# A hybrid attention and recurrence layer on one core: load order at the start, order of the gates, query blocks by twos, small products on both halves

## The chip, the cores and the metric

The kernel runs on one core of a Trainium2 chip. The metric is the time of one execution on the device, in microseconds (us), and less is better. TensorE (PE in the profile), VectorE (DVE), ScalarE (ACT), GpSimd (POOL) and SyncE (SP, which here only issues transfers) each work through a queue of their own and wait for each other through semaphores.

## What is computed

One layer of a decoder over 512 tokens of width 1024, all in float32. Cut to what matters here:

```python
xn = rmsnorm(x, norm_gain)
aq, ak, av, ag, bq, bf, bi, bg, gate_a, gate_b = split(xn @ w_in)      # 8 pieces of 512, 2 of 1024
q, k = rmsnorm(heads(aq)), rmsnorm(heads(ak))                          # 8 heads of 64
ya = softmax(q @ k.T / 8 + bias[q_pos - k_pos], causal) @ heads(av)    # 512 tokens: all blocks are selected
ya = (ya * silu(ag)) @ w_up_a
log_f, key = gates(bf)                                                 # 4 heads of 128
yb = gated_recurrence(q=silu(bq), k=key, v=bi, decay=log_f)
yb = (rmsnorm(yb) * silu(bg)) @ w_up_b
h = x + (sigmoid(gate_a) * ya + sigmoid(gate_b) * yb) @ w_out
out = h + (p @ w_ple) * sigmoid(h @ w_ple_gate)
```

## The kernel before

**The large products.** Every projection is three products of split operands. `split` (L183, L184) makes a high part on ACT and a low part on DVE, and `mm3` (L245) or `proj_tok` (L398) multiplies high by high, low by high and high by low, 512 columns each. Weights come through a ring: SP loads a raw tile (`wf`, 2 buffers), ACT writes `wh`, DVE writes `wl` (3 buffers each), two weights ahead of use. A new `wh` can be written only when TensorE is done with the tile whose buffer it takes. The first projection (`bi`) runs on x times its gain, before x is normalised, in four steps `start(kp)`. Its first weight comes in two halves (L269, L272), the second (`wf1`) whole.

**The side work.** Between the large products, the order of TensorE's queue is written out by the program itself (`manual_schedule` for PE). The generators of `sides` (`qk_norm`, `attention`, `recurrence`) yield an estimate of time, and `tick`, called after every group of large products, lets those that are due put their small products in. So each piece of side work interrupts the large products at a place that is fixed when the program is built. The queues of DVE and ACT are ordered by a planner from priorities, and some tiles are raised with `high_priority(offset=AHEAD)`.

**Attention.** `attention` walks through 16 steps, four query blocks of 128 tokens for each of four pairs of heads. `scores` (L641) writes two banks `s` of 128 x (128 to 512), six products on two 64-row halves. DVE adds the bias and takes the maximum (L648), ACT exponentiates (L650), DVE scales (L651, L652). `transposed` (L662) turns the result `p` through TensorE into `pt`, ACT copies it (L666), and after the last block `out_values` (L678) multiplies with the values. Only two banks of PSUM carry the tag `a` of all this, and `qk_norm` uses the same two for its transposes `qtp` and `ktp` (L623), which `scale_split` (L187 on ACT into `kh`, L188 on DVE into `kl`) empties.

**The recurrence.** `head(i)` makes `bf` and `bq` and then the gates (`hgrn_gates`, L423 to L441); in the kernel before all four heads' gates come before any output gate `ag`, `bg`. `hgrn_intra` writes one chunk's scores as a tree of levels 64, 32, 16, 8, 4, 2, 1. The 64-wide products (L494) all go to output rows 0 to 63, the 32-wide ones (L497, L498) to rows 96 to 127 and 64 to 95, and `diag` (L473) makes 16 products of 32 x 32 for each smaller level, of which only the later half of each pair of blocks is used: a mask in `pred` (L480) selects it. `hgrn_out` follows with transposes `hktp` (L538), states `hds` (L546), outputs `hop` (L559, L561) and a sum of squares `hms` (L572, L573), which needs the two parts `hth` (ACT) and `htl` (DVE).

Of the kernel before, what the change touches and what calls it, by code (L numbers as in the profile page):

```python
# [24 lines left out]
GH = 4  # L25
# [4 lines left out]

HP = 4.2
AP = 9.6
# [10 lines left out]
ORDER = [("ag", 0), ("bg", 0), ("bg", 1), ("ag", 1), ("gb", 0), ("gb", 1), ("gb", 2), ("bg", 2), ("ag", 2), ("gb", 3), ("gb", 4),  # L43
         ("gb", 5), ("bg", 3), ("ag", 3), ("ga", 0), ("ga", 1), ("gb", 6), ("gb", 7), ("ga", 4), ("ga", 2), ("ga", 3),
         ("ga", 5), ("ga", 6), ("ga", 7)] + [("ub", i) for i in range(KD)]
# [7 lines left out]
def hybrid_layer_kernel(  # L53
# [28 lines left out]
            "PT0": 2, "PT1": 2, "PT2": 2, "SG": 4, "YS": 1, "VV": 8, "s32": 1, "st": 1, "ps": 8}  # L82
# [109 lines left out]
    def w_sequence():  # L192
        for g in (2, 3, None, 0, 1):
            if g is None:
                wseq.extend([(w_tr[0], KD, 128), (w_tr[4], KD, 128)])
            else:
                wseq.extend((w_tok[g, kp], 2, 512) for kp in range(4))
        for i in range(1, GH):
            wseq.append((w_tr[i], KD, 128))
            wseq.append((w_tr[4 + i], KD, 128))  # L200
        for kind, i in ORDER:
            if kind == "ub":
# [59 lines left out]

    with tc.high_priority():

        x0 = unit("H", "xr0")
        xr.append(x0)
        raw0 = unit("w", "wf0", shape=(128, 2, 512))
        nc.sync.dma_start(x0[:, 0:256], xT[:, 0, 0:256])
# [152 lines left out]
    def hgrn_gates(h, F, Q):  # L421
        a = unit("H", f"ha{h}")
        A.activation(a, F, AF.Abs)  # L423
        A.activation(a, a, AF.Exp, scale=-1.0)
        A.activation(a, a, AF.Ln, bias=onec[:, 0:1])
        um = unit("H", f"hu{h}")
        V.tensor_scalar(um, F, -1.0, 30.0, op0=OP.mult, op1=OP.min)
        A.activation(um, um, AF.Exp)
        A.activation(um, um, AF.Ln, bias=onec[:, 0:1], scale=lbv[:, h:h + 1])
        V.scalar_tensor_tensor(a, F, 0.0, a, op0=OP.min, op1=OP.subtract)  # L430
        kb = unit("H", f"hk{h}")
        V.tensor_tensor(kb, a, F, op=OP.subtract)
        A.activation(kb, kb, AF.Exp, bias=ln1mlb[:, h:h + 1])
        G.tensor_tensor(a, a, um, op=OP.add)
        cum = um
        for c in range(NT):
            s_ = slice(c * 128, c * 128 + 128)
            V.tensor_tensor_scan(cum[:, s_], onec.to_broadcast([128, 128]), a[:, s_], 0.0, OP.mult, OP.add)
        q = a
        sigmoid(q, Q)  # L440
        V.tensor_tensor(q, q, Q, op=OP.mult)  # L441
        hg[h] = (kb, q, cum)

    def hgrn_intra(h):
# [24 lines left out]
        def diag(dst, l, r):  # L469
# [5 lines left out]
            cost(0.4)  # L475
# [3 lines left out]
        def pred(li, src):  # L479
            V.copy_predicated(s32, mk[:, li, None, :].to_broadcast([128, NT, 32]), src)  # L480
# [18 lines left out]
        cost(0.45)  # L499
# [4 lines left out]
        A.activation(sc[0:64, :, 64:128], big[0:64], AF.Copy)  # L504
        A.activation(sc[0:32, :, 32:64], big[96:128, :, 0:32], AF.Copy)
        A.activation(sc[64:96, :, 96:128], big[64:96, :, 0:32], AF.Copy)
# [6 lines left out]
        for i, k_ in enumerate(ks):  # L513
            diag(lpa[:, 1 + i], k_, k_)
# [85 lines left out]
    def qk_norm(name, banks, g, res):  # L600
# [19 lines left out]
        for i in range(HPAIRS):  # L620
            tp = bank("a", f"{name}tp{i}")
            for t in range(NT):
                PE.transpose(tp[:, t * 128:t * 128 + 128], raws[t][:, i * 128:i * 128 + 128], ident)  # L623
            cost(0.44)
            scale_split(hs[i], ls[i], tp, g)
            res.append((hs[i], ls[i]))
            yield 1.3
        done.add(name)

    def attention(qn, kn, va, sags, res):  # L630
        def scores(hp, qb, T):
            (qh, ql), (kh, kl) = qn[hp], kn[hp]
            nk = 128 * (qb + 1)
            qs = slice(qb * 128, qb * 128 + 128)
# [7 lines left out]
            cost(3 * max(0.107, nk * 0.00042))  # L642
            with tc.high_priority(offset=AHEAD):
                for j in range(2):
                    sp = sps[j]
                    pr = unit("P", f"p{hp}{qb}{j}")
                    st = unit("ps", f"ps{hp}{qb}{j}", shape=(128, 4))
                    V.tensor_tensor_reduce(pr[:, :nk], sp[:, :nk], T[j][:, nk - 1::-1], -1.0, 3e38,  # L648
                                           OP.add, OP.min, st[:, 0:1])
                    A.activation(pr[:, :nk], pr[:, :nk], AF.Exp, bias=st[:, 0:1], scale=-1.0, accum_out=st[:, 1:2])  # L650
                    V.reciprocal(st[:, 2:3], st[:, 1:2])  # L651
                    V.tensor_scalar(pr[:, :nk], pr[:, :nk], st[:, 2:3], None, op0=OP.mult)  # L652
# [3 lines left out]
        def transposed(hp, qb, prs):  # L656
            nk = 128 * (qb + 1)
            pts = []
            for j in range(2):
                tp = bank("a", f"pt{hp}{qb}{j}")  # L660
                for kb in range(qb + 1):
                    PE.transpose(tp[:, kb * 128:kb * 128 + 128], prs[j][:, kb * 128:kb * 128 + 128], ident)  # L662
                cost(0.11 * (qb + 1))
                pt = unit("PT" if qb == NT - 1 else f"PT{qb}", f"ptS{hp}{qb}{j}", shape=(128, nk))
                with tc.high_priority(offset=AHEAD):
                    A.activation(pt, tp[:, :nk], AF.Copy)  # L666
# [3 lines left out]
        def out_values(hp, pts):  # L670

            o = bank("a", f"o{hp}")
            for qb in range(NT):
                qs = slice(qb * 128, qb * 128 + 128)
                for kb in range(qb + 1):
                    for j in range(2):
                        h0 = hp * 128 + 64 * j
                        PE.matmul(o[64 * j:64 * j + 64, qs], va[kb][:, h0:h0 + 64],  # L678
                                  pts[qb][j][:, kb * 128:kb * 128 + 128], start=(kb == 0), stop=(kb == qb))
# [11 lines left out]
        steps = [(hp, qb) for hp in range(HPAIRS) for qb in range(NT)]  # L691
        T, prs, pts = {}, {}, {}
        for n in range(len(steps) + 2):
            if n >= 2 and steps[n - 2][1] == NT - 1:
# [3 lines left out]
                out_values(hp, [pts.pop(n - 2 - NT + 1 + i) for i in range(NT)])  # L698
            if n >= 2:
                yield AP * 0.3  # L700
            if 1 <= n <= len(steps):
                pts[n - 1] = transposed(*steps[n - 1], prs.pop(n - 1))
                yield AP * 0.3
            if n < len(steps):
                hp, qb = steps[n]
                if qb == 0:
# [6 lines left out]
                prs[n] = scores(hp, qb, [T[hp, 0], T[hp, 1]])  # L713
            yield AP * 0.4
# [8 lines left out]
    def start(kp):  # L723
        with tc.high_priority():
            if kp == 0:
                load_x(2, 3)
                first_splits()
                w_load(1)
                load_x(3, KD)
# [31 lines left out]
    for i in range(1, GH):  # L761
        head(i)

# [8 lines left out]
    for kind, i in ORDER:  # L772
        if kind == "bg":
# [134 lines left out]
```

## Time and profile before

| what | us |
|---|---|
| median of 3 runs (lowest, highest) | 488.33 (488.26, 488.42) |
| the profiled execution's own time | 488.94 |
| its span, first to last instruction | 487.2 |
| TensorE busy | 475.5 |
| VectorE busy | 301.5 |
| ScalarE busy | 266.6 |
| GpSimd busy | 30.4 |

The span is what the views of the profile cut up; the time of an execution is a little longer than its span. Busy times overlap between engines. Matmuls are pipelined, so a group of them is measured best from the start of the one before it to the start of the one behind it.

### The profile page before, as it was taken

What the parts mean: (1) busy time and instruction counts of PE and PEld (TensorE: products, weight loads), DVE (VectorE), ACT (ScalarE), POOL (GpSimd) and SP (SyncE); (2) the same over time, 40 slices, a digit from 0 to 9 for tenths busy, and PEclk for the clock granted to TensorE, in tenths of its full rate; (3) what the DMA queues carried; (4) which work ended last, traced back from release to release, by engine and by line L of the source; (5) the groups of instructions that cost most, each with busy time, mean ns of one, the idle gap of its engine ahead of it and who ended that gap; (6) DMA issues with size and microseconds to landing.
All of it is one profiled execution on the core that took longest, in us unless ns stands there. A gap on an engine that the chain in (4) does not pass through costs nothing.

```text
span 487.2 us, 7943 instructions
## 1 busy us (share of the span) xinstructions
PE 475.5 (98%) x3160; PEld 386.1 (79%) x3160; DVE 301.5 (62%) x596; ACT 266.6 (55%) x463; POOL 30.4 (6%) x43
## 2 busy tenths in 40 slices
PE   8999999999979999999999999999999999999996
PEld 6787888788757878777888788877888888888885
DVE  5849483858897966947449574364348855534332
ACT  6647573354876867758557785566324542242201
POOL 2004012103110001000100000000000000000000
PEclk9999999999999999999999999999999999999999
DMA  8432222422212131222212242014323544223211
GB/s 274 171 132 84 90 86 87 152 87 89 87 43 85 47 131 49 83 86 77 98 47 86 86 131 89 22 45 130 131 71 114 187 169 149 97 89 120 87 43 44
DMA packets 17941, 48.41 MB, mean 99 GB/s; under 512 B 2248, under 2 KB 2888, under 8 KB 17904
## 3 DMA queue, kind: packets, MB, share of 16 engines
q1 hardware_dynamic: 17616, 47.82, 28.9%
q8 instruction: 24, 0.39, 0.3%
q0 software_dynamic: 144, 0.09, 0.1%
q14 instruction: 13, 0.11, 0.1%
q10 hardware_dynamic: 144, 0.01, 0.0%
HBM read 45.79 MB, written 2.12 MB: 98 GB/s over the span
## 4 chain that ended last, share of the span: by engine, by line
PE 89%; DVE 5%; DMA 2%; ACT 2%; issue 1%; POOL 1%; SPq 0%; DVEq 0%; POOLq 0%
PE ga L245 9%; PE gb L245 9%; PE g L245 9%; PE h L245 9%; PE ak L398 5%; PE ag L245 5%; PE ub L245 5%; PE ua L245 4%; PE aq L398 4%; PE bg L245 4%; PE av L398 4%; PE bf L245 3%; PE bi L398 3%; PE bq L245 2%; PE pe L245 2%; PE s L641 2%
## 5 line engine op out<-in xcount | busy, mean ns | idle before, releaser
L183 ACT ACTIVATE wh<-wf 128x1024 fp32r<-128x1024 f32 (+1 forms) x81 | 78.1, 964 | 105.8 <-PE g L245 20.4
L184 DVE TENSOR_TENSOR wl<-wf,wh 128x1024 fp32r<-128x1024 f32 (+1 forms) x81 | 89.3, 1103 | 74.3 <-ACT wh L183 73.8
L245 PE MATMUL g<-hl,wh 128*128 128x512 f32 (+1 forms) x72 | 26.3, 366 | 0.0
L245 PE MATMUL g<-hh,wl 128*128 128x512 f32 (+1 forms) x72 | 26.3, 366 | 0.0
L245 PE MATMUL g<-hh,wh 128*128 128x512 f32 (+1 forms) x72 | 26.3, 366 | 0.0
L245 PE MATMUL gb<-xh,wh 128*128 128x512 f32 x64 | 26.3, 411 | 0.0
L245 PE MATMUL ga<-xh,wh 128*128 128x512 f32 x64 | 26.1, 408 | 0.0
L650 ACT ACTIVATE p<-p,ps 128x128 f32<-128x128 f32 (+3 forms) x32 | 17.7, 555 | 13.4 <-DVE ps L648 13.1
L245 PE MATMUL gb<-xl,wh 128*128 128x512 f32 x64 | 25.0, 391 | 0.0
L245 PE MATMUL ga<-xh,wl 128*128 128x512 f32 x64 | 25.0, 391 | 0.0
L245 PE MATMUL ga<-xl,wh 128*128 128x512 f32 x64 | 25.0, 391 | 0.0
L245 PE MATMUL gb<-xh,wl 128*128 128x512 f32 x64 | 25.0, 391 | 0.0
L245 PE MATMUL h<-ml,wh 128*128 128x512 f32 x64 | 24.9, 390 | 0.0
L245 PE MATMUL h<-mh,wl 128*128 128x512 f32 x64 | 24.9, 390 | 0.0
L245 PE MATMUL h<-mh,wh 128*128 128x512 f32 x64 | 24.9, 389 | 0.0
L666 ACT ACTIVATE ptS<-pt 128x128 f32<-128x128 f32 (+3 forms) x32 | 12.4, 435 | 14.8 <-PE pt L662 14.6
L648 DVE CUSTOM_DVE_ANT_0 p<-s,bias 128x128 f32<-128x128 f32 (+3 forms) x32 | 14.7, 487 | 7.0 <-PE s L641 7.0
L460 ACT ACTIVATE hx<-hx 128x512 f32<-128x512 f32 x24 | 14.6, 626 | 7.7 <-DVE hx L459 7.4
L806 DVE TENSOR_TENSOR hf<-h,xres 128x512 f32<-128x512 f32 x8 | 5.5, 692 | 18.1 <-PE h L245 18.1
L529 POOL COPY sc<-s 32x128 f32<-32x128 f32 x16 | 7.0, 435 | 142.9 <-DVE s L480 63.1
L245 PEld LDWEIGHTS g<-hl,wh 128*128 128x128 f32 x72 | 13.6, 189 | 2.2
L245 PEld LDWEIGHTS g<-hh,wl 128*128 128x128 f32 x72 | 13.6, 189 | 2.2
(326 smaller groups left out, 1267.0 us busy)
## 6 DMA issues: line engine op xcount, KB each, us to landing
wf<-in_w_tr_dram SPq DMA_DIRECT2D x32, 512.0 KB, 3.3
wf<-in_w_tok_dram SPq DMA_DIRECT2D x15, 512.0 KB, 3.4
wf<-in_w_up_dram SPq DMA_DIRECT2D x16, 256.0 KB, 2.6
wf<-in_w_o_dram SPq DMA_DIRECT2D x8, 512.0 KB, 3.3
wf<-in_w_g_dram SPq DMA_DIRECT2D x8, 512.0 KB, 3.4
bias<-ed SPq DMA_DIRECT2D x8, 256.0 KB, 3.7
xres<-in_xT_dram SPq DMA_DIRECT2D x8, 256.0 KB, 2.9
xr<-in_xT_dram SPq DMA_DIRECT2D x7, 256.0 KB, 6.3
```

What stands on the lines that cost most here:

```text
L183: A.activation(hi, src, AF.Copy)
L184: V.tensor_tensor(lo, src, hi.bitcast(F32), op=OP.subtract)
L245: PE.matmul(ps, a[:, k, :], b[k], start=(n == 0), stop=(n == tot - 1))
L398: PE.matmul(banks[t], a[:, s_], b[:, kk, :], start=(k == 0 and i == 0), stop=(k == KD - 1 and i == 2))
L460: A.activation(x, x, AF.Exp)
L529: G.tensor_copy(sc[s_, :, s_], s32[s_])
L641: PE.matmul(sps[j][:, :nk], a[js, qs], b[js, :nk], start=(i == 0), stop=(i == 2))
L648: V.tensor_tensor_reduce(pr[:, :nk], sp[:, :nk], T[j][:, nk - 1::-1], -1.0, 3e38, OP.add, OP.min, st[:, 0:1])
L650: A.activation(pr[:, :nk], pr[:, :nk], AF.Exp, bias=st[:, 0:1], scale=-1.0, accum_out=st[:, 1:2])
L666: A.activation(pt, tp[:, :nk], AF.Copy)
L806: V.tensor_tensor(t, ps, xres, op=OP.add)
```

## The change

**First loads.** SP's list at the start becomes: both halves of the first weight, then the third piece of x, the second weight, and the other pieces of x.

**Gates.** `ORDER` gets entries `("bf", i)`: heads 1 to 3 make `bf`, `bq` and their gates between the output gates. In `hgrn_gates` one sum goes from POOL to DVE, in `qk_norm` the squares go from POOL to ACT, and the split of `ktp` and `qtp` is raised in priority.

**Query blocks.** `STEPS` makes the first two query blocks one step: 12 steps instead of 16, and 384 columns of a bank hold both blocks.

**Small products.** The 64-wide products alternate between output rows 0 to 63 and 64 to 127, the 32-wide ones go through all four groups of 32 rows, and `diag` multiplies only the columns that the level uses (16 of 32). `pred` selects from that half alone, and the copies of the products out of PSUM become six instead of three.

```diff
+STEPS = ((0, 1), (2,), (3,))
-AP = 9.6
+AP = 12.8
-ORDER = [("ag", 0), ("bg", 0), ("bg", 1), ("ag", 1), ("gb", 0), ("gb", 1), ("gb", 2), ("bg", 2), ("ag", 2), ("gb", 3), ("gb", 4),
...
+ORDER = [("bg", 0), ("ag", 0), ("bf", 1), ("bg", 1), ("ag", 1), ("gb", 0), ("bf", 2), ("gb", 1), ("gb", 2), ("bg", 2), ("ag", 2),
+         ("gb", 3), ("bf", 3), ("gb", 4), ("gb", 5), ("bg", 3), ("ag", 3), ("ga", 0), ("ga", 1), ("gb", 6), ("gb", 7),
...
         nc.sync.dma_start(raw0[:, 1], wseq[0][0][:, 1])
-        wraw.append(raw0)
+        load_x(2, 3)
+        w_load(1)
+        load_x(3, KD)
...
-        G.tensor_tensor(a, a, um, op=OP.add)
+        V.tensor_tensor(a, a, um, op=OP.add)
...
+        def queries(t, b):
+            return t.rearrange("p (n two b) -> p n two b", two=2, b=b)[:, :, 1, :]
-                    PE.matmul(dst[32 * g:32 * g + 32, c, :], l[:, o:o + 32], r[:, o:o + 32],
-                              start=True, stop=True)
+                    d, m = dst[32 * g:32 * g + 32, c, :], r[:, o:o + 32]
+                    if b:
+                        d, m = queries(d, b), queries(m, b)
+                    PE.matmul(d, l[:, o:o + 32], m, start=True, stop=True)
...
-            o = c * 128
-            PE.matmul(big[0:64, c, :], k64[:, o:o + 64], k64[:, o + 64:o + 128], start=True, stop=True)
+            o, i = c * 128, 64 * (c % 2)
+            PE.matmul(big[i:i + 64, c // 2, :], k64[:, o:o + 64], k64[:, o + 64:o + 128], start=True, stop=True)
         for c in range(NT):
-            o = c * 128
-            PE.matmul(big[96:128, c, 0:32], k32[:, o:o + 32], k32[:, o + 32:o + 64], start=True, stop=True)
-            PE.matmul(big[64:96, c, 0:32], k32[:, o + 64:o + 96], k32[:, o + 96:o + 128], start=True, stop=True)
+            for half in range(2):
+                o, i = c * 128 + 64 * half, 64 * (c % 2) + 32 * half
+                PE.matmul(big[i:i + 32, 2 + c // 2, 0:32], k32[:, o:o + 32], k32[:, o + 32:o + 64], start=True, stop=True)
...
-        diag(lpb[:, 0], k1, k1)
-        diag(lpa[:, 0], k16, k16)
+        diag(lpb[:, 0], k1, k1, 1)
+        diag(lpa[:, 0], k16, k16, 16)
...
-            G.tensor_tensor(sq, raw, raw, op=OP.mult)
+            A.activation(sq, raw, AF.Square)
...
-            scale_split(hs[i], ls[i], tp, g)
+            with tc.high_priority(offset=AHEAD):
+                scale_split(hs[i], ls[i], tp, g)
...
-            sps = [bank("a", f"s{hp}{qb}{j}") for j in range(2)]
-            for i, (a, b) in enumerate(((qh, kh), (ql, kh), (qh, kl))):
-                for j in range(2):
-                    js = slice(64 * j, 64 * j + 64)
-                    PE.matmul(sps[j][:, :nk], a[js, qs], b[js, :nk], start=(i == 0), stop=(i == 2))
+            sps = [bank("a", f"s{hp}{qbs[0]}{j}") for j in range(2)]
+            for qb, o, nk in blocks(qbs):
+                qs = slice(qb * 128, qb * 128 + 128)
+                for i, (a, b) in enumerate(((qh, kh), (ql, kh), (qh, kl))):
+                    for j in range(2):
+                        js = slice(64 * j, 64 * j + 64)
+                        PE.matmul(sps[j][:, o:o + nk], a[js, qs], b[js, :nk], start=(i == 0), stop=(i == 2))
...
         for kind, i in ORDER:
-            if kind == "bg":
+            if kind == "bf":
+                head(i)
+            elif kind == "bg":
```

What moves in the queues is seen best in two places. The first is SP at the start of the program (`xr` is a piece of x, `wf` a raw weight). Before:

```order
L270 DMA xr_100<-in_xT_dram 128x256
L137 DMA xr_105<-in_xT_dram 128x512
L137 DMA xr_119<-in_xT_dram 128x512
L272 DMA wf_101<-in_w_tok_dram 128x512
L219 DMA wf_137<-in_w_tok_dram 128x1024
L137 DMA xr_139<-in_xT_dram 128x512
```

With the change:

```order
L272 DMA xr_100<-in_xT_dram 128x256
L139 DMA xr_105<-in_xT_dram 128x512
L274 DMA wf_101<-in_w_tok_dram 128x512
L139 DMA xr_108<-in_xT_dram 128x512
L220 DMA wf_110<-in_w_tok_dram 128x1024
L139 DMA xr_112<-in_xT_dram 128x512
```

The second half of the first weight and the third piece of x change places; what comes ahead of the second weight is the same in sum. ACT's list there, with the change (`gh` is the high part of a piece of x, `ssum` and `xsq` its squares):

```order
L189 ACTIVATE gh_143<-xr_105,sm 128x512
L185 ACTIVATE wh_135<-wf_101 128x512
L189 ACTIVATE gh_186<-xr_108,sm 128x512
L181 ACTIVATE lb<-lb 128x4
L309 ACTIVATE ssum<-xr_100 128x512
L312 ACTIVATE xsq_337<-xr_105 128x512
L312 ACTIVATE xsq_340<-xr_108 128x512
L185 ACTIVATE wh_154<-wf_110 128x1024
```

Before, `gh` of the third piece stood ahead of `wh` of the half weight, and the other rows were the same: the squares of three pieces stand ahead of the second weight's `wh` in both.

The second place is DVE's list from the third `kl` to the first scores. Before:

```order
L188 SCALAR_TENSOR_TENSOR kl_1138<-ktp_1334,sm,kh_1134 128x512
L184 TENSOR_TENSOR wl_1357<-wf_1354,wh_1356 128x1024
L261 TENSOR_TENSOR hy_1237<-hy_1237,ht_1238 128x512
L427 TENSOR_SCALAR hu_1432<-bf_1293 128x512
L188 SCALAR_TENSOR_TENSOR kl_1139<-ktp_1347,sm,kh_1135 128x512
L430 SCALAR_TENSOR_TENSOR ha_1428<-bf_1293,ha_1428 128x512
```

With the change:

```order
L190 SCALAR_TENSOR_TENSOR kl_1141<-ktp_1323,sm,kh_1137 128x512
L593 SCALAR_TENSOR_TENSOR ho_1241<-hop_1233,sm,hy_1242 128x512
L186 TENSOR_TENSOR wl_1346<-wf_1343,wh_1345 128x1024
L431 TENSOR_SCALAR hu_1418<-bf_1290 128x512
L599 TENSOR_TENSOR bg0s<-bg0s,ho_1241 128x512
L190 SCALAR_TENSOR_TENSOR kl_1142<-ktp_1336,sm,kh_1138 128x512
L434 SCALAR_TENSOR_TENSOR ha_1414<-bf_1290,ha_1414 128x512
L186 TENSOR_TENSOR ybl_1273<-bg0s,ybh_1272 128x512
L436 TENSOR_TENSOR hk_1423<-ha_1414,bf_1290 128x512
L671 ISA p_1374,ps_1375<-s_1360,bias_1356 128x128
```

Between the last two `kl` three rows stood, now four stand; the `hu` row is of the second head's gates (`bf1`), which were the third head's before. Further ahead, DVE's list no longer has the second head's gates between the states `st` and `htl`: there stands only `bg0s`, one product.

## Rows read from the trace of the kernel before

**Rows 1.** The page: busy us of each engine, share of the span, instructions.

```profile
PE 475.5 (98%) x3160; PEld 386.1 (79%) x3160; DVE 301.5 (62%) x596; ACT 266.6 (55%) x463; POOL 30.4 (6%) x43
```

**Rows 2.** Busy time by stretch: length, then each engine's busy us.

```profile
110.00:140.00 30.00, 27.43 (x229) 21.94 (x227) 26.49 (x54) 21.05 (x34) 5.64 (x8) 1.00 0.21 72
140.00:152.00 12.00, 10.02 (x49) 7.58 (x50) 10.07 (x28) 7.17 (x16) 1.29 (x1) 1.00 0.25 88
```

**Rows 3.** TensorE's waits from 100 to 160 us: total, times, longest.

```profile
PE s L641 <- DVE kl L188: 1.7, 1, 1.7
PE pt L662 <- DVE p L652: 1.2, 2, 0.7
PE hms L573 <- DVE htl L184: 1.2, 1, 1.2
PE ktp L623 <- DVE kl L188: 0.5, 1, 0.5
```

**Rows 4.** Timeline of the start: start, us, engine, instruction, [idle before, releaser].

```profile
8.56 0.63 ACT L183 ACTIVATE wh<-wf 128x512 fp32r<-128x512 f32 x1 [0.44 <-DMA wf<-in_w_tok_dram]
9.24 0.50 PE L398 MATMUL bi<-wh,gh 128*128 128x512 f32 x1 [0.68 <-ACT wh L183]
9.71 1.14 ACT L308 ACTIVATE xsq<-xr 128x512 f32<-128x512 f32 x2
10.76 1.05 ACT L183 ACTIVATE wh<-wf 128x1024 fp32r<-128x1024 f32 x1
11.83 1.23 DVE L184 TENSOR_TENSOR wl<-wf,wh 128x1024 fp32r<-128x1024 f32 x1
```

**Rows 5.** Timeline of DVE and ACT, 126 to 141 us.

```profile
126.91 1.37 DVE L438 TENSOR_TENSOR_SCAN hu<-onec,ha 128x128 f32<-128x128 f32 x4 [1.65 <-POOL ha L434]
128.19 0.67 DVE L184 TENSOR_TENSOR htl<-ht,hth 128x512 fp32r<-128x512 f32 x1
...
137.65 1.22 DVE L184 TENSOR_TENSOR wl<-wf,wh 128x1024 fp32r<-128x1024 f32 x1
...
139.98 0.75 DVE L188 SCALAR_TENSOR_TENSOR kl<-ktp,sm,kh 128x512 fp32r<-128x512 f32 x1
```

**Rows 6.** Timeline of PE around a 128-column and a 256-column run of scores.

```profile
293.98 0.39 PE L245 MATMUL ga<-xh,wl 128*128 128x512 f32 x1
...
294.46 0.28 PE L641 MATMUL s<-kh,ql 64*128 64x128 f32 x2
294.57 0.28 PE L641 MATMUL s<-kl,qh 64*128 64x128 f32 x2
...
295.11 0.39 PE L245 MATMUL ga<-xl,wh 128*128 128x512 f32 x1
...
150.53 0.39 PE L245 MATMUL bf<-xh,wl 128*128 128x512 f32 x1
...
151.74 0.40 PE L245 MATMUL bf<-xl,wh 128*128 128x512 f32 x1
```

**Rows 7.** The chain that ended last: start, us, the large products of `ua`.

```profile
362.52 21.76 PE ua L245 x96
```

**Rows 8.** Timeline of PE, small products of the first head.

```profile
92.45 0.68 PE L494 MATMUL lpb<-hx 128*64 128x64 f32 x8
...
93.14 0.20 PE L497 MATMUL lpb<-hx 128*32 128x32 f32 x1
93.15 0.20 PE L498 MATMUL lpb<-hx 128*32 128x32 f32 x1
93.17 0.20 PE L497 MATMUL lpb<-hx 128*32 128x32 f32 x1
...
93.89 0.45 PE L473 MATMUL lpa<-hx 128*32 128x32 f32 x30
```

**Rows 9.** Timeline of PE: products with 1 and with 128 moving columns, full weights.

```profile
32.35 0.95 PE L322 MATMUL mt<-onesd,ssum 128*128 128x1 f32 x8
...
118.90 0.83 PE L546 MATMUL hds<-biv,hkt 128*128 128x128 f32 x6
```

More of the change, by code (lines that the diff above doesn't have):

```diff
@@ L197, in w_sequence @@
                 wseq.extend((w_tok[g, kp], 2, 512) for kp in range(4))
-        for i in range(1, GH):
-            wseq.append((w_tr[i], KD, 128))
-            wseq.append((w_tr[4 + i], KD, 128))
         for kind, i in ORDER:
-            if kind == "ub":
+            if kind == "bf":
+                wseq.extend([(w_tr[i], KD, 128), (w_tr[4 + i], KD, 128)])
+            elif kind == "ub":
                 wseq.append((w_up[i, 1], 4, 128))
@@ L513, in hgrn_intra @@
         for i, k_ in enumerate(ks):
-            diag(lpa[:, 1 + i], k_, k_)
+            diag(lpa[:, 1 + i], k_, k_, LEVELS[1 + i])
         kd = unit("KT", f"hkd{h}")
@@ L630, in attention, with blocks, scores @@
     def attention(qn, kn, va, sags, res):
-        def scores(hp, qb, T):
+        def blocks(qbs):
+            return [(qb, sum(128 * (b + 1) for b in qbs[:i]), 128 * (qb + 1)) for i, qb in enumerate(qbs)]
+        def scores(hp, qbs, T):
             (qh, ql), (kh, kl) = qn[hp], kn[hp]
-            nk = 128 * (qb + 1)
-            qs = slice(qb * 128, qb * 128 + 128)
             prs = []
-            sps = [bank("a", f"s{hp}{qb}{j}") for j in range(2)]
-            for i, (a, b) in enumerate(((qh, kh), (ql, kh), (qh, kl))):
-                for j in range(2):
-                    js = slice(64 * j, 64 * j + 64)
-                    PE.matmul(sps[j][:, :nk], a[js, qs], b[js, :nk], start=(i == 0), stop=(i == 2))
-            cost(3 * max(0.107, nk * 0.00042))
+            sps = [bank("a", f"s{hp}{qbs[0]}{j}") for j in range(2)]
[5 more added lines that the diff above has]
+                        PE.matmul(sps[j][:, o:o + nk], a[js, qs], b[js, :nk], start=(i == 0), stop=(i == 2))
+                cost(3 * max(0.107, nk * 0.00042))
@@ L651, in scores @@
-                    V.reciprocal(st[:, 2:3], st[:, 1:2])
-                    V.tensor_scalar(pr[:, :nk], pr[:, :nk], st[:, 2:3], None, op0=OP.mult)
+                    pr = unit("P", f"p{hp}{qbs[0]}{j}")
+                    for qb, o, nk in blocks(qbs):
+                        p_ = pr[:, o:o + nk]
+                        st = unit("ps", f"ps{hp}{qb}{j}", shape=(128, 4))
+                        V.tensor_tensor_reduce(p_, sps[j][:, o:o + nk], T[j][:, nk - 1::-1], -1.0, 3e38,
+                                               OP.add, OP.min, st[:, 0:1])
+                        A.activation(p_, p_, AF.Exp, bias=st[:, 0:1], scale=-1.0, accum_out=st[:, 1:2])
+                        V.reciprocal(st[:, 2:3], st[:, 1:2])
+                        V.tensor_scalar(p_, p_, st[:, 2:3], None, op0=OP.mult)
@@ L653, in scores, with transposed @@
                     prs.append(pr)
             return prs
-        def transposed(hp, qb, prs):
-            nk = 128 * (qb + 1)
+        def transposed(hp, qbs, prs):
+            n = sum(qb + 1 for qb in qbs)
             pts = []
             for j in range(2):
-                tp = bank("a", f"pt{hp}{qb}{j}")
-                for kb in range(qb + 1):
+                tp = bank("a", f"pt{hp}{qbs[0]}{j}")
+                for kb in range(n):
                     PE.transpose(tp[:, kb * 128:kb * 128 + 128], prs[j][:, kb * 128:kb * 128 + 128], ident)
-                cost(0.11 * (qb + 1))
-                pt = unit("PT" if qb == NT - 1 else f"PT{qb}", f"ptS{hp}{qb}{j}", shape=(128, nk))
+                cost(0.11 * n)
+                pt = unit("PT" if n == NT else f"PT{qbs[0]}", f"ptS{hp}{qbs[0]}{j}", shape=(128, n * 128))
@@ L672, in out_values @@
             o = bank("a", f"o{hp}")
[L673 to L679, printed above, removed]
+            for qbs, pt in zip(STEPS, pts):
+                for qb, o0, nk in blocks(qbs):
+                    qs = slice(qb * 128, qb * 128 + 128)
+                    for kb in range(qb + 1):
+                        for j in range(2):
+                            h0 = hp * 128 + 64 * j
+                            PE.matmul(o[64 * j:64 * j + 64, qs], va[kb][:, h0:h0 + 64],
+                                      pt[j][:, o0 + kb * 128:o0 + kb * 128 + 128], start=(kb == 0), stop=(kb == qb))
             cost(1.5)
@@ L690, in attention @@
             yield lambda: {"q", "k"} <= done
-        steps = [(hp, qb) for hp in range(HPAIRS) for qb in range(NT)]
+        NS = len(STEPS)
+        steps = [(hp, i) for hp in range(HPAIRS) for i in range(NS)]
         T, prs, pts = {}, {}, {}
         for n in range(len(steps) + 2):
-            if n >= 2 and steps[n - 2][1] == NT - 1:
+            if n >= 2 and steps[n - 2][1] == NS - 1:
                 hp = steps[n - 2][0]
@@ L697, in attention @@
                     yield lambda: f"ag{hp}" in done
-                out_values(hp, [pts.pop(n - 2 - NT + 1 + i) for i in range(NT)])
+                out_values(hp, [pts.pop(n - 1 - NS + i) for i in range(NS)])
             if n >= 2:
```

53 lines of the change are left out of this document (25 added, 28 removed).

## The prediction

> **What bounds the kernel now.** I read the page first: TensorE is busy 475.5 us of the span, VectorE 62% of it, ScalarE 55%, GpSimd 6% [rows 1]. So time is saved in two ways only: TensorE gets less to do, or it waits less. Next, the busy time by stretch, to see where it waits. From 110 to 152 us it is busy 27.43 of 30 and 10.02 of 12 us, that is 4.5 us idle, and there VectorE is the full engine, with 26.49 and 10.07 us [rows 2]. TensorE's waits of that stretch name four causes, 4.6 us in all, each of them VectorE [rows 3]. The timeline of the first microseconds shows the other waits. Last I measured what one interruption of the large products costs, from the start of the large product before it to the start of the second one behind it, because a large product that follows a small one starts slower. Undisturbed, one large product takes 21.76 / 96 = 0.227 us [rows 7].
>
> The sum is made against the profiled execution's 488.94 us. It lies 0.6 us above the median of the three runs, 488.33, so 0.6 us is taken off at the end.
>
> **First loads.** The wait removed is plain: TensorE stood 0.68 us before the second half weight's first product, since `wh` of that half began at 8.56, right when its load landed [rows 4]. With the third piece of x behind it, it lands earlier. But I cost this at nothing, because of what is late next. The next products need `wl` of the second weight, and that ends at 11.83 + 1.23 = 13.06. Ahead of it, ACT's list holds the squares of three pieces of x (the last two at 9.71, for 1.14 us) and then `wh` at 10.76, for 1.05 us. The change keeps that order. The third square now waits for a piece of x that lands later, about when the half weight landed before, so ACT is not done sooner. What TensorE gains at 9.24 it waits for again at 13. The ends: 0.7 us gained, if ACT gets ahead all the same, and 0.3 us lost, if the late piece pushes the squares back. I take 0.
>
> **Two query blocks in one run.** TensorE multiplies the same columns. What goes is one run of scores and one run of transposes per pair of heads. The 128-column run costs 295.11 - 293.98 = 1.13 us less two large products, 0.45, that is 0.68; the 256-column run 151.74 - 150.53 = 1.21 less 0.45, that is 0.76 [rows 6, 7]. Joined, they cost the second run and three more pairs of 128-column products at 0.11 us (294.46 to 294.57), 1.09 us in place of 1.44. Four times 0.35 is **1.4 us saved**. The transposes are as many as before and as wide as the stream; a run fewer of them, and a score run that no longer shares its switch with a run of the recurrence, are small and of opposite signs, so I leave them at nothing (0.3 us either way). ACT copies `pt` 24 times instead of 32, which hides beside TensorE.
>
> **Products on both halves.** The 64-wide products are eight records in 0.68 us (an fp32 product is recorded twice). Less the last one's 0.22, which I estimate from the 0.20 us of the 32-wide ones, that is 0.46 us in seven gaps, 0.066 us each. The 32-wide ones go to two output groups in turn, two records in 0.03 us. The products of a level go through four groups: 30 records in 0.45 - 0.20 = 0.25 us, 0.0086 us each [rows 8]. So a record costs the same time per group, 0.03 us, and groups run side by side. On two halves I take half of 0.46 (0.23 saved), on four groups 16 records at 0.0086 in place of 0.015 (0.11 saved): 0.34 us for each of four heads, **1.4 us saved**. The ends are 0, if the halves don't overlap, and these 1.4.
>
> The Trainium skill (TensorE: Matmul & The Clock Gate, Part 3: Packing small matmuls, The mechanism) says that weight loads overlap with running matmuls only when the row group differs. By that rule this term would be 0, since both halves use all 128 rows, and the time 485.0 us. The rows just read speak against it: four groups with the same 128 rows run at a quarter of the gap of one.
>
> **Half of the columns in `diag`.** Five levels in four heads, 20 times 32 records, now move 16 columns in place of 32. At one end the gap halves: 640 x 0.0043 = 2.7 us saved. At the other it stays. The nearest rows are products with full weights: with one moving column eight records take 0.95 us, 0.12 each; with 128 columns six take 0.83 us, 0.14 each [rows 9]. Moving 128 times fewer columns takes a seventh off. What stays must be the weights, which are loaded for each record, and `diag` loads the same weights as before. I take **0**. `pred` on DVE gets shorter, the copies of `sc` on ACT become six for three; neither is waited for.
>
> **The gates and what moves off POOL.** This is the term on waits. `hms` waited 1.2 us for `htl` [rows 3]. `htl` started at 128.19, behind the second head's scan, which itself had waited 1.65 us for POOL's sum [rows 5]. The gates no longer stand there, and the sum is on DVE: this wait goes. The 0.5 us at `ktp` were DVE's full queue as well: it goes.
>
> The 1.7 us at the first scores stay. These scores need both banks of tag `a`, that is the third and the fourth `kl`. Before, `wl` started at 137.65 and the fourth `kl` at 139.98, 2.33 us later, with `wl`, `hy` and `hu` between [rows 5]. Now `wl`, `hu` and `bg0s` stand there, of the same sizes, and `ho` ahead of them: one more row, some 0.6 us. TensorE asks for the banks as late as before, six large products after the last `ktp`. So I expect 2.3 us. The fourth `kl` is raised in priority, but in the queue it still stands behind them.
>
> The 1.2 us at `pt` shrink. Nine more large products stand between scores and transposes, 9 x 0.227 = 2.0 us, while DVE gets a second block's rows and the sum `ha`. I take 0.4. Together 2.7 in place of 4.6 us: **1.9 us saved**. The ends: all waits go, 4.6 saved; or only those at `hms` and `ktp` go and the one at the scores grows, 1.1 saved.
>
> What is moved past others: head 1's weights now come behind `bg0` and `ag0` in the ring, and SP loads them in the order of use as before. The squares of `qk_norm` go to ACT, eight more activations, while ACT idles 45% of the span; the transposes that need them come 14 us of the program's own clock later, and rows 3 name no wait for them. The later heads' recurrence starts later, but 39 large products, 8.9 us, stand between its last `hms` and the products `ub` that need it.
>
> **The sum.** 0 + 1.4 + 1.4 + 0 + 1.9 = 4.7 us. 488.94 - 4.7 - 0.6 = **483.6 us**.
>
> **The rivals.**
> - The half columns pay: 2.7 us more, 480.9 us. For it: 32 columns and 32 weights are as long as each other, so either could set the gap. Against it: rows 9. Chance 0.15.
> - The middle waits stay at 4.6 us, since gates of the second head now meet the first softmax on DVE: 483.6 + 1.9 = 485.5 us. For it: VectorE is full there [rows 2], and its queue is written from estimates. Against it: two of the four waits lose their cause. Chance 0.16.
> - The halves don't overlap: 483.6 + 1.4 = 485.0 us. Against it: rows 8. The rule cited above from the Trainium skill (the same page and section) is this case. Chance 0.08.
> - Slower: each move of the output from one half to the other drains the array. Ten moves a head, 40 in all. The price of a drain by rows 6: of the 0.68 us of the 128-column run 0.33 are products, and 0.35 are the way in and out, 0.17 each. 40 x 0.17 = 6.8 us, and the 1.4 are not gained: 483.6 + 1.4 + 6.8 = 491.8 us. It would decide from 3.3 / 40 = 0.08 us a move. Against it: the 32-wide products change groups at every record within 0.01 us [rows 8]. Chance 0.04.
>
> **How the numbers follow.** Forecast 0.52, half columns 0.15, waits 0.16, halves 0.08, drains 0.04, and 0.05 for several of the lesser gains failing together, which leaves under 1 us. A measurement of this kernel can tell about 0.2%, 1.0 us, from no change. The first four cases are faster by more than that: 0.91 faster, 0.05 the same, 0.04 slower. The range runs from a little under the half columns' case, 480.6, up to 486.2, between the waits' case, 485.5, and waits and halves failing together, 486.9.
>
> **What would show it.** Scores in 12 runs; the joined run near 1.1 us. The 64-wide products at 0.03 us a record. A level's 30 records still at 0.25 us: at 0.13 the half columns pay. TensorE's waits near the second gates: none at `hms`, some 2.3 us at the first scores for `kl`. At the start no wait at 9 us and one before 13.4 for `wl`. The prediction is wrong if TensorE's idle time in the middle isn't near 2.7 us, or if the start is shorter by over 0.5 us.

## The result, and the profile after

The changed kernel takes 483.53 us (median of 4, 483.31 to 483.64) beside 488.38 us (488.26 to 488.55) before: a ratio of 0.990, with a 95% interval of 0.9883 to 0.9917. The profiled execution took 483.52 us, its span is 481.7 us. The forecast of 483.6 us holds, but not all of its terms: the one on waits came out near by errors of opposite sign, and the one on the half columns is right for another reason than it gave.

The page of the changed kernel: busy times, and the granted clock in 40 slices.

```profile
PE 473.3 (98%) x3160; PEld 386.9 (80%) x3160; DVE 300.8 (62%) x600; ACT 269.8 (56%) x475; POOL 14.1 (3%) x31
...
PEclk9999999999989999999999999999999999999999
```

Beside [rows 1], TensorE is 2.2 us less busy and GpSimd half as busy; the rest went out of waits. One slice of the clock, around 139 us, has an 8. The busy time by stretch (columns as in [rows 2]; the sixth number after the stretch's length, the one behind POOL's, is the clock):

```profile
110.00:140.00 30.00, 28.05 (x241) 22.96 (x239) 24.28 (x43) 21.07 (x35) 1.16 (x4) 0.99 0.26 89
140.00:152.00 12.00, 12.00 (x51) 9.64 (x53) 11.13 (x38) 9.05 (x22) 0.00 (x0) 0.88 0.13 39
```

TensorE is idle 1.95 us there, after 4.5 before. But in the second stretch the granted clock is 0.88. TensorE's waits in the whole span of the changed kernel:

```profile
PE s L663 <- DVE kl L190: 2.0, 1, 2.0
...
PE bi L402 <- DVE wl L186: 0.7, 2, 0.5
PE bi L402 <- ACT wh L185: 0.3, 1, 0.3
...
```

Of the four waits of [rows 3] one is left, at the first scores. The timeline of TensorE around it, and what follows:

```profile
138.87 0.32 PE L663 MATMUL s<-kh,qh 64*128 64x128 f32 x1 [1.95 <-DVE kl L190]
...
139.88 0.79 PE L246 MATMUL bq<-xh,wh 128*128 128x512 f32 x1
140.47 0.63 PE L246 MATMUL bq<-xl,wh 128*128 128x512 f32 x1
140.90 0.63 PE L246 MATMUL bq<-xh,wl 128*128 128x512 f32 x1
...
143.00 0.39 PE L246 MATMUL bq<-xl,wh 128*128 128x512 f32 x1
143.23 0.39 PE L246 MATMUL bq<-xh,wl 128*128 128x512 f32 x1
```

Behind the wait the large products start 0.43 us apart, nearly twice the usual 0.227, and from 143.0 on 0.23 again. The busy time by shorter stretches shows the clock:

```profile
139.80:143.30 3.50, 3.50 (x10) 2.73 (x10) 3.50 (x17) 2.66 (x10) 0.00 (x0) 0.55 0.00 0
143.30:148.00 4.70, 4.70 (x25) 3.91 (x24) 4.70 (x17) 3.00 (x6) 0.00 (x0) 1.00 0.02 5
```

A granted clock of 0.55 is the lower level, 1.2 GHz, for most of 3.5 us. The 27 products behind the scores start 1.53 us later than at 0.227 us each; behind other runs of scores it is 0.13 us. So the fall costs 1.4 us.

The timeline of the start (answers to [rows 4]):

```profile
8.06 0.63 ACT L185 ACTIVATE wh<-wf 128x512 fp32r<-128x512 f32 x1
8.74 0.50 PE L402 MATMUL bi<-wh,gh 128*128 128x512 f32 x1 [0.29 <-ACT wh L185]
9.96 1.14 ACT L312 ACTIVATE xsq<-xr 128x512 f32<-128x512 f32 x2
11.00 1.04 ACT L185 ACTIVATE wh<-wf 128x1024 fp32r<-128x1024 f32 x1
12.08 1.23 DVE L186 TENSOR_TENSOR wl<-wf,wh 128x1024 fp32r<-128x1024 f32 x1
13.36 0.50 PE L402 MATMUL bi<-wl,gh 128*128 128x512 f32 x1 [0.52 <-DVE wl L186]
```

TensorE goes on 0.5 us earlier, at 8.74, behind a wait of 0.29 us, but the squares, `wh` and `wl` of the second weight are each 0.25 us later. The product that needs this `wl` waits 0.52 us for it and starts at 13.36, before the change at 13.11.

The timeline of TensorE at three more places: the small products of the first head (answers to [rows 8]), the run of 96 records of three levels with the large products beside it, and a joined run of scores (answers to [rows 6]):

```profile
92.44 0.39 PE L402 MATMUL ak<-wl,xh 128*128 128x512 f32 x1
92.76 0.45 PE L507 MATMUL lpb<-hx 128*64 128x64 f32 x8
93.14 0.33 PE L511 MATMUL lpb<-hx 128*32 128x32 f32 x16
...
93.88 0.43 PE L485 MATMUL lpa<-hx 128*32 128x16 f32 x30
94.24 0.50 PE L402 MATMUL ak<-wh,xh 128*128 128x512 f32 x1
...
112.38 0.39 PE L402 MATMUL ak<-wl,xh 128*128 128x512 f32 x1
112.70 1.00 PE L485 MATMUL lpa<-hx 128*32 128x16 f32 x96
113.63 0.50 PE L246 MATMUL bg<-xh,wh 128*128 128x512 f32 x1
...
182.37 0.39 PE L246 MATMUL gb<-xh,wl 128*128 128x512 f32 x1
...
183.58 0.50 PE L246 MATMUL gb<-xh,wh 128*128 128x512 f32 x1
183.91 0.39 PE L246 MATMUL gb<-xl,wh 128*128 128x512 f32 x1
```

Eight 64-wide records take 0.45 instead of 0.68 us. Thirty records with half the columns take 0.43 instead of 0.45. The joined run takes 183.91 - 182.37 - 0.45 = 1.09 us, the forecast's number.

From here on a run of small products is costed as the start of the first large product behind it, less the start of the large product before it, less 0.227 us. So the interrupted rhythm is in it, and waits are too. The first head's run costs 94.24 - 92.44 - 0.227 = 1.58 us.

### The profile page after: what moved, and what is told of

The parts are those of the page before. It is cut to its first block, busy times and chain, and to the rows that moved or that the text cites. A ratio compares the mean times of both kernels' runs of the same rounds, so it can differ in the third digit from the quotient of the medians.

```text
span 481.7 us, 7941 instructions
## 1 busy us (share of the span) xinstructions
PE 473.3 (98%) x3160; PEld 386.9 (80%) x3160; DVE 300.8 (62%) x600; ACT 269.8 (56%) x475; POOL 14.1 (3%) x31
## 4 chain that ended last, share of the span: by engine, by line
PE 92%; DVE 4%; ACT 1%; DMA 1%; issue 1%; SPq 0%; DVEq 0%
PE gb L246 9%; PE ga L246 9%; PE g L246 9%; PE h L246 9%; PE bg L246 5%; PE ak L402 5%; PE bq L246 5%; PE ub L246 5%; PE ua L246 5%; PE aq L402 5%; PE ag L246 4%; PE av L402 4%; PE bf L246 3%; PE pe L246 2%; PE bi L402 2%; PE s L663 2%
## 5 line engine op out<-in xcount | busy, mean ns | idle before, releaser
L689 ACT ACTIVATE ptS<-pt 128x384 f32<-128x384 f32 (+1 forms) x24 | 11.6, 521 | 7.4 <-PE pt L685 7.2
L246 PEld LDWEIGHTS g<-hh,wh 128*128 128x128 f32 x72 | 13.6, 189 | 2.2
```

Of the source, the lines that this page charges most:

```text
L246: PE.matmul(ps, a[:, k, :], b[k], start=(n == 0), stop=(n == tot - 1))
L689: A.activation(pt, tp[:, :n * 128], AF.Copy)
```

## The experiments

The theory after these readings: every part is worth what the prediction says, the order of the gates makes the term on waits, the load order costs 0.3 us, and the one wait left costs more than itself through the clock. Its rivals: the halves or the joined blocks gave less and the waits more; the move of work off GpSimd, not the order, took the waits away; the half columns pay.

All the kernels are the changed one with one edit. Each result is listed with the mean clock granted to TensorE in each execution, because the fall just seen comes in some executions of a program and not in others.

**The changed kernel again.**

> The changed kernel itself, again, beside the three below on the same chip. Theory (the clock falls after the wait at the first scores in some executions and not in others): executions with a mean granted clock of 1.000 are about 1.5 us shorter than those at 0.996, near 482 us against 483.5. Rival (the clock is a matter of each program): all executions at 0.996, 483.5 within 0.3.

483.15 us (482.46 to 483.84), ratio 0.9889 (0.9876 to 0.9903). The execution at a mean clock of 0.999 took 482.46, the profiled one at 0.995 took 483.84, with 1.1 us lost behind a 1.9 us wait. Of the other two one took 483.61 at 0.995, but one only 482.7 at 0.996, so the mean clock doesn't order them fully. One kernel spreads over 1.4 us, more than most of the parts that are to be told apart, and below the traces count more than the medians.

**The query blocks one by one.**

```diff
-STEPS = ((0, 1), (2,), (3,))
-AP = 12.8
+STEPS = ((0,), (1,), (2,), (3,))
+AP = 9.6
...
-            "PT0": 2, "PT2": 2, "SG": 4, "YS": 1, "VV": 8, "s32": 1, "st": 1, "ps": 8}
+            "PT0": 2, "PT1": 2, "PT2": 2, "SG": 4, "YS": 1, "VV": 8, "s32": 1, "st": 1, "ps": 8}
```

> The changed kernel with four query blocks as four steps again, the rest as changed. Theory (a run of scores costs TensorE 0.35 us of switching besides its products): four runs more, 483.5 + 1.4 = 484.9 us, between 484.5 and 485.5 since the middle waits may shift; the 128-column run costs 0.68 us and the 256-column run 0.76, against 1.09 for the joined one. Rival (the whole gain came from the waits between 110 and 152 us, and interruptions hide): 483.5 within 0.3.

484.51 us (484.11 to 485.37), ratio 0.9921 (0.9905 to 0.9938). The four executions' clocks are 0.994 to 1.000; those at 0.999 and 1.000 took 484.1 to 484.8, some 2 us above the changed kernel's 482.46 (this trace also has 0.6 us of waits for `p`). In the trace a 128-column run costs 0.57 and a 256-column run 0.64 us, the joined one 0.98; with the 0.11 that the large product behind each loses the joining gains 0.34 us, four times, where the forecast had 0.35. The two-block transposes cost 0.58 us joined, 0.14 and 0.36 apart, and the large product behind each run loses 0.09: joined or apart is the same within 0.01 us.

**The products on one half.** The 64- and 32-wide products and their copies as before the change (one row for three):

```diff
-            PE.matmul(big[i:i + 64, c // 2, :], k64[:, o:o + 64], k64[:, o + 64:o + 128], start=True, stop=True)
+            PE.matmul(big[0:64, c, :], k64[:, o:o + 64], k64[:, o + 64:o + 128], start=True, stop=True)
```

> The changed kernel with the 64-wide products all on output rows 0 to 63 and the 32-wide ones on two groups, as before. Theory (a group of output rows takes 0.03 us a record of 32 columns, and groups run side by side): the first run of a head goes from 1.58 back to 1.91 us, four times 0.33, 484.8 us. Rival (waits alone): 483.5 within 0.3.

484.16 us (483.09 to 485.41), ratio 0.9909 (0.9889 to 0.9929). The medians alone would leave it open: executions at clocks of 0.995 to 1.000 overlap the changed kernel's. The run doesn't. TensorE at the first head's run in this kernel:

```profile
92.08 0.39 PE L402 MATMUL ak<-wl,xh 128*128 128x512 f32 x1
...
94.20 0.50 PE L402 MATMUL ak<-wh,xh 128*128 128x512 f32 x1
```

It costs 1.90 us where the changed kernel has 1.58, and the fourth head's 1.89 and 1.58. The second head's run is joined with scores and the third's with transposes: 2.79 against 2.48, and 2.79 against 2.47. So it is 0.31 to 0.32 us in all four. The wait at the scores is 2.0 us in both. So the halves do run side by side. By the rule of the Trainium skill (TensorE: Matmul & The Clock Gate, Part 3: Packing small matmuls, The mechanism), by which weight loads overlap only across row groups, there would have been no difference here. The measurement decides.

**All 32 columns, and half the weights.** The first passes no `b` to `diag`. The second loads 16 weight columns for the five levels, so their other 16 rows of scores are missing, and leaves out the copies by `pred`:

```diff
-                    PE.matmul(d, l[:, o:o + 32], m, start=True, stop=True)
+                    if b:
+                        PE.matmul(queries(dst[32 * g:32 * g + 16, c, :], b), l[:, o:o + 16], m, start=True, stop=True)
...
-        pred(4, lpb[:, 0])
```

> The changed kernel with all 32 columns in every small level, of which half are not used. Theory (the weights of each record set its gap, not the moving columns): 483.5 within 0.3 us, and 96 records of a run still cost about 1.02 to 1.05 us. Rival (columns set the gap): up to 2.7 us more, 486.2 us.

483.49 us (483.02 to 484.76), ratio 0.9899 (0.9883 to 0.9915): no difference, so the 2.7 us of the rival are out. That the totals agree this closely is chance: this profile shows no fall of the clock, but a start 0.5 us longer and 1.1 us lost at a wait for `ptS` (ACT's copy of `pt`). The run decides: the 96 records cost 1.05 us with 32 columns, 1.02 with 16.

> The small products of the five levels load 16 weight columns in place of 32 and move 16, so that only 16 of the 32 keys of a block are taken; the rows that this would leave unset are not read, the copies of the small levels into the score tile are left out. If the weights set the gap of these products, the run of 96 records gets shorter than the changed kernel's 1.02 us: halving the gaps of 0.0086 us takes 96 x 0.0043 = 0.41 us off, to some 0.6 us. If something for each record sets it, whatever its size, the run stays within 0.05 us of 1.02. Its total is not compared, since VectorE does less.

TensorE in the kernel with half the weights:

```profile
111.68 0.39 PE L402 MATMUL ak<-wl,xh 128*128 128x512 f32 x1
112.00 0.96 PE L486 MATMUL lpa<-hx 128*16 128x16 f32 x96
112.89 0.50 PE L246 MATMUL bg<-xh,wh 128*128 128x512 f32 x1
```

From 111.68 to 112.89 it is 1.21 us, from 112.38 to 113.63 in the changed kernel 1.25: the run costs 0.98 instead of 1.02 us, not 0.6. So between 16 and 32 neither the moving columns nor the weights set the gap; a record has a price of its own, 0.0086 us with four groups in turn. The Trainium skill (TensorEngine Tiling (Array Packing), Instruction Overhead) says that a matmul with one moving column takes as long as one with 60. The runs with 32 and with 16 columns, 1.05 and 1.02 us, agree.

**The gates first, and the work back on GpSimd.** The first puts heads 1 to 3's `bf` ahead of the output gates again; the second gives the sum and the squares back:

```diff
-ORDER = [("bg", 0), ("ag", 0), ("bf", 1), ("bg", 1), ("ag", 1), ("gb", 0), ("bf", 2), ("gb", 1), ("gb", 2), ("bg", 2), ("ag", 2),
-         ("gb", 3), ("bf", 3), ("gb", 4), ("gb", 5), ("bg", 3), ("ag", 3), ("ga", 0), ("ga", 1), ("gb", 6), ("gb", 7),
+ORDER = [("bf", 1), ("bf", 2), ("bf", 3), ("ag", 0), ("bg", 0), ("bg", 1), ("ag", 1), ("gb", 0), ("gb", 1), ("gb", 2), ("bg", 2), ("ag", 2),
+         ("gb", 3), ("gb", 4), ("gb", 5), ("bg", 3), ("ag", 3), ("ga", 0), ("ga", 1), ("gb", 6), ("gb", 7),
```

> The changed kernel with the gates of heads 1 to 3 ahead of all output gates again. Theory (the order took away the waits at hms and ktp, with some 1.8 us): about 485.3 us, TensorE's waits between 110 and 152 us back above 3.5 us. Rival (those waits went because POOL's work went to DVE and ACT): 483.5 within 0.5, and no wait at hms.

```diff
-    V.tensor_tensor(a, a, um, op=OP.add)
+    G.tensor_tensor(a, a, um, op=OP.add)
...
-            A.activation(sq, raw, AF.Square)
+            G.tensor_tensor(sq, raw, raw, op=OP.mult)
```

> The sum of the gates and the squares of q and k go back to GpSimd, the order of the gates stays as the change has it. If the order of the gates alone takes the wait for the column sum away, there is still none at hms, the waits of the middle stay near 2 us, and the time is within 0.5 us of the changed kernel at an equal clock (483 to 484). If the sum's move to VectorE did it, the scan waits for GpSimd again (1.65 us before) and the wait at hms comes back with some 1.2 us: near 485.

The old order: 486.33 us (485.89 to 487.91), ratio 0.9956 (0.9941 to 0.9971), and in its trace TensorE waits:

```profile
PE s L663 <- DVE kl L190: 3.1, 1, 3.1
...
PE ktp L640 <- DVE kl L190: 1.0, 1, 1.0
...
PE hms L590 <- DVE htl L186: 0.3, 1, 0.3
```

The sum and the squares on GpSimd: 485.38 us (484.0 to 486.23), ratio 0.9919 (0.9891 to 0.9948), clocks 0.992 to 0.996, and TensorE's waits in its trace are

```profile
PE s L663 <- DVE kl L190: 2.0, 1, 2.0
...
PE s L663 <- ACT ptS L689: 0.6, 1, 0.6
```

With the new order alone there is no wait at `hms` or `ktp`. With the old order, and the sum on VectorE, there are 4.4 us of waits, nearly as many as before, moved to the scores. The first `hms` doesn't wait in either kernel (the 0.3 us are at a later head's), so its wait alone doesn't tell the order from the sum. The total of the waits does: it is small with the new order only, 2.6 us against 4.4, so the order makes this term. The median with GpSimd is some 2 us above the changed kernel's, and not within the 0.5 us expected. In the profiles that is the clock, 2.4 us lost behind the wait in place of 1.1 or 1.4, and the wait for `ptS`, by which the third pair's joined run takes 1.93 us in place of 0.98. Whether GpSimd's work brings either stays open: the kernel with all 32 columns waits for `ptS` as well.

**The first loads as before, and the squares of x on GpSimd.**

```diff
-        load_x(1, 2)
+        load_x(1, 3)
         nc.sync.dma_start(raw0[:, 1], wseq[0][0][:, 1])
-        load_x(2, 3)
         w_load(1)
```

> The changed kernel with the first loads in the order of before. Theory (the wait before the half weight moved to the low part of the second weight, and the squares on ScalarE set that): the time of the changed kernel within 0.3 us, rather 0.3 shorter; the low part of the second weight done at about 13.1 us instead of 13.3. Rival (the new order pays by itself): 0.7 us longer.

483.46 us (482.0 to 484.93), ratio 0.9898 (0.9879 to 0.9916). Its five executions run from 482.0 at a clock of 0.999 to 484.93 at 0.993, so the medians say nothing. The trace is 0.4 us ahead of the changed kernel's second profile at 33 us, and 0.25 ahead of its first.

The other tests the reason, that ScalarE's squares hold back the second weight's split: the squares of the first three pieces and their sums go to GpSimd.

> The changed kernel with the squares of the first three pieces of x, and their sums, on GpSimd instead of ScalarE and VectorE. Theory (those squares stand ahead of the second weight's split and eat what the new load order wins): the split of the second weight starts at its landing, near 10.1 us in place of 11.0, and TensorE has about 0.8 us less to wait before 14 us, 482.7 us. Rival (VectorE's low parts set the pace of the start anyway, or GpSimd slows VectorE): 483.5 within 0.3.

485.80 us (484.79 to 486.64), ratio 0.9942 (0.9928 to 0.9956): slower, and the start is 2.1 us longer. The timelines of DVE and of POOL:

```profile
8.25 1.61 DVE L190 SCALAR_TENSOR_TENSOR gl<-xr,sm,gh 128x512 fp32r<-128x512 f32 x1
9.78 1.23 DVE L180 TENSOR_SCALAR lb<-lb 128x4 f32<-128x4 f32 x1
...
7.09 2.22 POOL L313 TENSOR_TENSOR xsq<-xr 128x512 f32<-128x512 f32 x2
9.27 3.48 POOL L314 TENSOR_TENSOR ssum<-ssum,xsq 128x512 f32<-128x512 f32 x2
```

While GpSimd squares and adds, VectorE's `gl` takes 1.61 us instead of 0.75 and a row of four elements a partition 1.23 instead of 0.16. ScalarE's row ahead of the second weight's `wh` waits 2.28 us for that one, so `wh` starts at 11.15 us and not at the 10.1 expected. The Trainium skill (SBUF — State Buffer, Terms) says that VectorE and GpSimd share a pair of ports that one instruction holds alone; the two slow rows of this trace agree. So the experiment didn't test the reason: it brought a larger cost.

**The first scores later, then the first transposes too.** The wait at the scores should go if they are asked for later. First the scores alone, then with the transposes and the old first loads, then the same with the change's first loads:

```diff
             yield lambda: {"q", "k"} <= done
+        yield 2.7
         NS = len(STEPS)
...
                 hp, i = steps[n - 1]
+                if n == 1:
+                    yield 2.5
                 pts[n - 1] = transposed(hp, STEPS[i], prs.pop(n - 1))
```

> The changed kernel with all of attention's steps 12 large products (2.7 us) later behind the transposes of k. Theory (TensorE waits 2.0 us at the first scores for the fourth low part of k, and its clock falls behind that wait): both go, 483.5 - 2.0 - 1.4 = about 480.1 us, no wait at the scores, granted clock 1.000. Rival (VectorE is the limit there, and the wait comes back at the transposes of the first softmax or later): 482 us or more.

483.51 us (482.05 to 483.78), ratio 0.9898 (0.9883 to 0.9913). No gain, so this expectation fell. The wait at the scores is gone from its trace, and TensorE's waits now have

```profile
PE pt L685 <- DVE p L675: 2.5, 2, 1.5
```

The scores were put later in TensorE's queue, the transposes were not. Without the wait and the fall TensorE reached the transposes at 145.6 us instead of 147.3, of which 0.6 us come from a shorter start. VectorE began with `p` at 139.91 instead of 140.53, the same 0.6 us sooner, but was done with it later: the planner put a weight's `wl` (1.20 us) and the second head's rows ahead of the last scaling.

> The order of first loads of before, the first scores 2.7 us of the program's clock later, and the first transposes 2.5 us later still. If the waits at the first scores and then at the first transposes are only VectorE's queue being asked too early, both go (2.0 and 2.5 us in the runs so far), no second wait appears, and the clock has no cause to fall: TensorE waits only at the start, and the time is 483.2 - 2.0 - 0.3 = 480.9 us at the same clock, some 479.5 where the clock doesn't fall. If VectorE's total work up to that place sets the end, the wait moves on, to the copies for lpb or to the second scores, with some 2 us, and the time stays at 483.

**480.06 us** (479.95 to 481.0), ratio 0.9822 (0.9803 to 0.9841): faster than both kernels. TensorE's waits behind the start (total, times, longest), and the busy time by stretch around the first scores:

```profile
PE ub L246 <- DVE ybl L186: 0.2, 1, 0.2
PE ub L246 <- ACT ybh L185: 0.2, 1, 0.2
...
```

```profile
136.50:139.80 3.30, 3.30 (x24) 2.49 (x23) 3.30 (x9) 2.44 (x5) 0.00 (x0) 1.00 0.46 159
139.80:143.30 3.50, 3.50 (x17) 2.89 (x16) 3.50 (x18) 3.29 (x11) 0.00 (x0) 1.00 0.02 5
```

VectorE is as full as before, TensorE doesn't wait, and the clock stays: 0.998 to 1.000 in all four executions. A small wait is new, at `ub` near 330 us; with the slower start of the products beside it, it takes 1.0 us back. The time lies between the 480.9 and the 479.5 us expected.

> As the kernel with both moved later, but with the first loads in the change's order: the one difference between the two is the first loads, without the clock's falls in the middle that spread the other comparisons. If the change's order costs 0.3 us or gives nothing, as forecast, the time is 480.0 to 480.4, and TensorE waits for the second weight's low part before 13.4 us. If that order gains its 0.7 us, it is near 479.4. Under both the middle has no wait over 0.3 us, and the granted clock stays at 0.998 or more.

481.03 us (480.64 to 482.19), ratio 0.9856 (0.984 to 0.9872), clocks 0.998 to 1.000. Here, without falls, the first loads can be compared: 1.0 us between the medians (on two chips, the ratios' intervals just touch), and in the traces the products behind `mp` begin at 33.09 us instead of 32.42. The timeline of ScalarE up to the second weight's `wh`, first with the change's loads, then (second fence) in the kernel with the old ones:

```profile
8.37 0.73 ACT L189 ACTIVATE gh<-xr,sm 128x512 fp32r<-128x512 f32 x1
...
9.61 1.14 ACT L312 ACTIVATE xsq<-xr 128x512 f32<-128x512 f32 x2
10.66 1.04 ACT L185 ACTIVATE wh<-wf 128x1024 fp32r<-128x1024 f32 x1
```

```profile
6.46 1.38 ACT L189 ACTIVATE gh<-xr,sm 128x512 fp32r<-128x512 f32 x2 [0.16 <-DMA xr<-in_xT_dram]
...
8.94 1.14 ACT L311 ACTIVATE xsq<-xr 128x512 f32<-128x512 f32 x2
9.98 1.04 ACT L185 ACTIVATE wh<-wf 128x1024 fp32r<-128x1024 f32 x1
```

With the old loads both `gh` run in one piece from 6.46; with the change's the third piece's `gh` comes at 8.37, behind the half weight, and the squares and `wh` are 0.67 us later. The expectation, 480.0 to 480.4, was too low. The traces give 0.7 us, the medians 1.0.

The other traces show what of this is fixed. In the ten profiles with the change's loads and the squares on ScalarE the second weight's `wh` starts 2.94 to 3.05 us behind the half weight's, in the three with the old loads 2.19 to 2.20: some 0.75 us, as long as the `gh` that now stands between them. But the half weight's `wh` itself starts anywhere from 7.42 to 8.51 us with the change's loads and from 7.79 to 8.56 with the old ones. So one pair of profiles doesn't give the net effect: it was 0.26 us between the two kernels and 0.67 here.

## Why the prediction was right

- **First loads, 0 forecast.** The mechanism held, TensorE waits before 13.4 us for `wl` as said, but the term was mis-sized: 0.3 us lost (first `av` at 29.72 us, before at 29.46), and 0.7 to 1.0 us in the pair without falls. The third piece's `gh`, 0.73 us on ScalarE, moved behind the half weight and pushes the squares back. The prediction had this only as an end of 0.3, with the piece's landing as the reason.
- **Joined query blocks, 1.4 us.** 4 x 0.34, and next to nothing from the transposes. Right.
- **Both halves, 1.4 us.** 1.91 - 1.58 = 0.33 us for the first head, 1.3 us for four. Right, and the rival in which they don't overlap fell; so did the one of drains, since the run got shorter.
- **Half columns, 0.** 1.05 - 1.02 = 0.03 us a run, 0.1 in all. The number was right by luck, the step to it wrong: "What stays must be the weights" fell with the half weights.
- **Waits, 1.9 us.** Near in sum, by errors of opposite sign. The wait at the scores is 2.0 us by the wait rows (2.3 forecast) and the one at `pt` gone (0.4 forecast), so the idle time in the middle is 1.95 us and not the 2.7 that the prediction named as its sign. The price of the old waits was too low as well. `hms` before the change, as an example:

```profile
127.12 0.39 PE L245 MATMUL bq<-xh,wl 128*128 128x512 f32 x1
...
128.92 0.50 PE L573 MATMUL hms<-htl,ones 128*128 128x512 f32 x1 [1.17 <-DVE htl L184]
129.25 0.40 PE L245 MATMUL bf<-xh,wh 128*128 128x512 f32 x1
```

This run costs 129.25 - 127.12 - 0.227 = 1.91 us, undisturbed 0.46, so the wait costs 1.45 where its row says 1.2. By runs, the others cost 0.72 at `ktp`, 2.02 at `s` and 1.63 at `pt`, 5.8 us in all in place of 4.6; a wait row counts from the modelled end of the product before, 0.39 us from its start, though the next could start after 0.227. The changed kernel has 2.41 left. A second `hms`, at 254 us, lost 0.56 more before and nothing now. That is 4.0 us gained. Then the fall of the clock, which the prediction didn't foresee, took 1.4 back: 2.6 us.

The sum is 0.3 - 1.4 - 1.3 - 0.1 - 2.6 = -5.1 us; the last large product starts 5.0 us earlier (477.25 against 482.26). The forecast was -4.7, and the medians differ by 4.85. The spans of the two profiles differ by 0.5 more than the 5.0 us: that lies behind the last large product, 4.94 us to the end before and 4.45 after.

What the changed kernel still had to give was mostly one cause: VectorE's fourth `kl` was asked for too early. Asked for later, with the transposes behind it, neither the wait at the scores nor the fall of the clock is there: the mean clock is 0.998 or more in all eight executions of the last two kernels, whose scores and transposes both come later.

## What to carry to other kernels

A wait of the engine that bounds the kernel has to be priced from the start of the product before it to the rhythm regained behind it, not by its row of idle time alone; here that was 5.8 us for 4.6, and the lower clock behind the one that was left 1.4 more. A piece of side work that waits can be moved back in the bound engine's queue at little cost (here 1.0 us came back at `ub`), but what hangs on it must be moved as well: the scores alone gave nothing, scores and transposes some 2 us with the same first loads (481.03 against 483.15, on two chips), 3 with the old ones. And when terms of a few tenths are in question, take away first what makes executions differ.

## What was not expected of the hardware

- Behind a wait of 1.9 to 3.1 us the granted clock fell to the lower level (0.50 in one stretch of 3 us with the old order of gates) in some executions and not in others of the same program. The products behind it lost 1.1 to 2.4 us. The profiles of the kernel before (a wait of 1.7 us), of the one-by-one blocks and of all 32 columns (2.0 us each) show none.
- Small float32 products with 32 columns and 32 weights, 16 and 32, or 16 and 16 cost nearly the same, some 0.0086 us a record (1.05, 1.02 and 0.98 us for a run of 96), measured with four output groups in turn.
- While GpSimd squared and added, VectorE's `gl` took twice its time (1.61 us for 0.75), and a row of four elements a partition nearly eight times (1.23 for 0.16).
